# Gathers one expert earlier in the queue, roots by a power on GpSimd, and another order of the last norm, in a hybrid decoder trunk

## The chip, the cores and the metric

The kernel runs on one core of one Trainium2 chip. The metric is the device time of one execution in microseconds (us), lower is better. PE is TensorE, DVE is VectorE, ACT is ScalarE, POOL is GpSimd, and SP is SyncE, which here only starts DMAs.

## The reference

One layer over 1024 tokens of 1024 channels: a token mixer, a cross-attention to 256 memory tokens, and a mixture of 16 experts of which each token uses two; a last RMSNorm stands behind. The change touches the norms, the experts and the last norm:

```
def rmsnorm(x, g):
    xf = x.astype(jnp.float32)
    y = xf * lax.rsqrt(jnp.mean(xf * xf, axis=-1, keepdims=True) + EPS)
    return (y * g.astype(jnp.float32)).astype(x.dtype)
...
    weight = g_val * e_val
    eid = g_idx * EXPERTS_PER_GROUP + e_idx
    gate = jnp.sum(jax.nn.one_hot(eid, N_EXPERTS, dtype=jnp.float32) * weight[..., None], axis=1)
    act = jax.nn.silu(jnp.einsum('nd,edf->nef', t, w_e_gate)) * jnp.einsum('nd,edf->nef', t, w_e_up)
    act = act * gate[:, :, None].astype(act.dtype)
    out = jnp.einsum('nef,efd->nd', act, w_e_down)
...
        x = x + gated_branch_mixer(h, w_in[l], conv_a_w[l], conv_a_b[l], ln_a_g[l], ln_a_b[l],
                                   w_a_out[l], w_pool_grp[l], pool_scale[l], conv_c_w[l],
                                   w_c_out[l], w_o[l])
        x = x + memory_cross_attention(rmsnorm(x, norm_x_g[l]), rmsnorm(mem, norm_mem_g[l]),
                                       w_xq[l], w_xkv[l], w_xo[l])
        x = x + hierarchical_moe(rmsnorm(x, norm_ffn_g[l]), w_rg[l], b_rg[l], w_re[l], b_re[l],
                                 w_e_gate[l], w_e_up[l], w_e_down[l])
    return rmsnorm(x, norm_f_g)
```

## The kernel before

All matrix products take float32 operands apart into a high and a low part (`wh` and `wl`, `xh` and `xl`, `aTh` and `aTl`) and add three products. A weight tile comes by SP's queue as `raw`; ACT casts it to `wh` (L114) and DVE, for a few tiles POOL, subtracts to `wl` (L117). These splits go in the order of one list, and `split_to(n)` in the text says how far at that place; `load_to(n)` does the same for the loads. Instructions run on each engine in the order in which the text issues them; nothing is rescheduled.

**Up to about 1050 us** the mixer and the attention run in tiles of 128 tokens, PE nearly without a gap. The norms' square root (`rstd_of`, L166) is a guess by a shift on integers and three Newton rounds, of small operations on DVE or POOL. The last token tile's norm (`add_half`, L1079, and the lines below it) feeds the router, whose choices give each expert its list of tokens (`toki`) and their number (`cnti`).

**Experts.** They run in a fixed order. Expert e has a first block of up to 128 tokens and, where its count is above 128, a second block in the If branch at L1408. The token rows come by an indirect DMA on POOL (`gather_rows`, L1153) from `t_d` into a slot of `merged`. PE transposes them (`xe`, or `xb` for a second block, L1182), ACT and DVE split the transposed rows (`xh`, `xl`), PE multiplies by the gate and up weights (`gu`, or `gub`, 24 matmuls, L1197), ACT and DVE form silu(gate) times up (`sg`, L1255 and L1256), PE transposes that (`at`, L1291), ACT and DVE split it (`aTh`, `aTl`), PE multiplies by the down weights (`y`, `yb`), ACT and DVE scale the result by the token's weight into one of three y slots of `merged` (L1304, L1306), and an indirect DMA of POOL adds those rows to `x2_d` in memory (`add_rows`, L1157). Each scatter-add waits until the one before it has landed. While expert e runs its gate and up products, DVE does six `wl` of a later expert; `next_in(e)` then transposes the rows of expert e+1. `gather_both(e + 3)` stands behind the branch of expert e, and so behind the scatter-adds of that branch on POOL. Five slots hold gathered rows in turn.

**The last two experts and the last norm.** Experts 14 and 15 don't add to memory. After the last scatter-add of expert 13 the eight 128-token tiles of `x2_d` are loaded by SP (`nat`, L1324), squared and summed on ACT (L1328), scaled on DVE (L1336) and written out; the rows of tokens that experts 14 and 15 use are gathered (`rows_in`), get the experts' result added on DVE (`final_add`, L1351), are squared (L1352), scaled (L1361) and written by an indirect DMA over those of `nat` (`rows_out`, L1345). `HOOKS` is a table of which of these steps runs at which place of expert 14 (key -2) and expert 15 (key -1): "end" is behind the expert, "act" behind the transposes of `sg`, "put" behind the result of the expert before, "gate" behind `sgb`, "act1" behind the transposes of `sgb`.

Of the kernel before, what the change touches and what calls it, by code (L numbers as in the profile page):

```python
# [9 lines left out]
F32 = mybir.dt.float32  # L10
# [9 lines left out]
P = 128  # L20
D = 1024
# [108 lines left out]
def kernel(ctx: ExitStack, tc: tile.TileContext, x, mem, rows, cols, w_in, w_ac,  # L130
# [34 lines left out]

    def rstd_of(ss, name, n=1, unit=None, y=None, base=EPS):  # L166
        unit = unit or dve
        pool = small if y is None else mo
        v = pool.tile([P, NT], F32, tag="v", bufs=2, name=f"v_{name}")[:, :n]
        q = pool.tile([P, NT], F32, tag="q", bufs=2, name=f"q_{name}")[:, :n]  # L170
        if y is None:
            y = pool.tile([P, NT], F32, tag="y", bufs=2, name=f"y_{name}")[:, :n]
        yi = y.bitcast(I32)
        dve.tensor_scalar(v, ss, 1.0 / D, base, op0=OP.mult, op1=OP.add)
        dve.tensor_scalar(yi, v.bitcast(I32), 1, None, op0=OP.logical_shift_right)
        dve.tensor_scalar(yi, yi, -1, 0x5F3759DF, op0=OP.mult, op1=OP.add)
        unit.tensor_scalar(v, v, -0.5, None, op0=OP.mult)
        for _ in range(3):
            if n == 1:
                unit.tensor_scalar(q, y, v, y, op0=OP.mult, op1=OP.mult)  # L180
                unit.tensor_scalar(y, q, 1.5, y, op0=OP.add, op1=OP.mult)
            else:
                unit.tensor_tensor(q, y, v, op=OP.mult)
                unit.tensor_tensor(q, q, y, op=OP.mult)
                unit.tensor_scalar(q, q, 1.5, None, op0=OP.add)
                unit.tensor_tensor(y, q, y, op=OP.mult)
        return y
# [69 lines left out]
    def prep_rstd(b, n):  # L257
        rstds[b] = rstd_of(sums[b], b, n, unit=dve if b == "m" else pool_e)

# [861 lines left out]

    SLOTS = {"x": (3, 4, 5, 6, 7), "y": (0, 1, 2), "f": (0, 1, 2, 5)}
    mslots = {"x": 0, "y": 0, "f": 0}

# [44 lines left out]

    def gather_both(e):  # L1170
        if e:
            gather(e, 0)
# [86 lines left out]
    def gate_up_out(e, ps):  # L1259
        ast.split_to(EW + 6 * e + (8 if e else 10))  # L1260
        ast.load_to(EW + 6 * e + 23)
        if e == 0:
            gather_both(2)
        return act_of(ps, f"{e}")

    def next_in(e, ps):
        xs = xs_tile(f"{e + 1}")
        x_in(xg[e + 1, 0], ps, xs)
        return xs

    sg = gate_up_out(0, gu0)
    xs1 = xs_tile("0b")
# [57 lines left out]
    def norm_rstd(t0, t1):  # L1330
        rstd_of(nsum[:, t0:t1], f"n{t0}", t1 - t0, pool_e, nrstd[:, t0:t1])

# [15 lines left out]
    def final_add(ps, e, b):  # L1348
        for h in range(2):
            f = fin[e, b][:, h * 512:(h + 1) * 512]  # L1350
            dve.scalar_tensor_tensor(f, ps[h], w_of_slot(e, b), f, op0=OP.mult, op1=OP.add)  # L1351
            act.activation(fjunk[:, 0:512], f, AF.Square, accum_out=fsum[:, e - NF, b, h:h + 1])  # L1352

    def final_rstd(e, b, unit):
        ss = fsum[:, e - NF, b]
        dve.tensor_tensor(ss[:, 0:1], ss[:, 0:1], ss[:, 1:2], op=OP.add)
        rstd_of(ss[:, 0:1], f"f{e}_{b}", 1, unit, frstd[:, e - NF, b:b + 1])

# [4 lines left out]
    def put(ps, e, b):  # L1363
        if e < NF:
            y_out(ps, e, b)
        else:
            final_add(ps, e, b)
            if b and e < E2:
                final_rstd(e, b, dve)
                final_scale(e, b)  # L1370
# [7 lines left out]
    def first_rows_out():  # L1378
# [15 lines left out]
    for e in range(NE):  # L1394
# [13 lines left out]
        with tc.If(count_of(e, CALC_P + [ET.SP] if end else CALC_P) > P) as cmp:  # L1408
            x_in(xg[e, 1], bank_pair(f"xb{e}"), xs1)
            if last:  # L1410
                down(yps, *last, 0, (0,))
            if e >= NF:
                rows_in(e, 1)
            act_tr(sg, pa, aT)
            hook(e, "act")
            if last and own:
                down(yps, *last, 0, (1,))
                down(yps, *last, 1)
                put(yps, e - 1, 0)
# [210 lines left out]
```

## Time and profile before

| | |
|---|---|
| median of 3 runs | 1354.13 us (1353.12 to 1354.61) |
| the profiled execution: time, span | 1349.84 us, 1348.2 us |
| busy: PE, DVE, ACT, POOL | 1268.7, 811.1, 447.6, 144.9 us |
| mean granted clock of TensorE | 0.974 |
| 100 to 1057 us: PE busy | 946.01 of 957.00 us |
| 1264.7 to 1282.7 us (expert 13): PE busy | 13.59 of 18.00 us |
| 1282.7 to 1294.3 us (expert 14): PE busy | 7.39 of 11.60 us |
| 1321.1 to 1348.2 us (behind PE's end): DVE busy, POOL busy | 13.79 of 27.10, 7.00 of 27.10 us |

The profiled execution is one other than the three timed ones. Its span is what the traces measure; 1.64 us of its time lie around the span. Share of busy time says little by itself: from 100 to 1057 us PE is full, and behind 1321 us it has nothing left to do.

### The profile page before, as it was taken

The numbers are of one execution on the slowest core, as the hardware profiler recorded it, in microseconds if no ns is written. First come the engines' busy times: TensorE is split into PE (matmuls) and PEld (weight loads), VectorE is DVE, ScalarE is ACT, GpSimd is POOL, SyncE is SP. The second block draws the span as 40 slices with busy tenths as digits, with TensorE's granted clock in tenths as the row PEclk, the third lists the DMA queues.
The fourth block names the chain that finished last, engine by engine and source line by source line (L and its number), as shares of the span: only waits on it lengthen the run. The fifth ranks groups of instructions, "written<-read, shape, count | busy, mean of one in ns | idle before, by whom it ended". The sixth has DMA issues, their size and how long they took to land. (4 is left out here: it accounts for less than half of the span.)

```text
span 1348.2 us, 16066 instructions
## 1 busy us (share of the span) xinstructions
PE 1268.7 (94%) x6150; PEld 1054.2 (78%) x6151; DVE 811.1 (60%) x1210; ACT 447.6 (33%) x611; POOL 144.9 (11%) x157
## 2 busy tenths in 40 slices
PE   7999999999999999999999999999999689998871
PEld 7988888888888888888888898887888477776661
DVE  5836787887874356322344554335777767657665
ACT  6511221221111133212132253435312456555571
POOL 2400000000000000000000020011000423212243
PEclk8999999999999999999999999999999799999986
DMA  7641111121111112111153240113434788979773
GB/s 290 214 145 47 39 63 32 52 78 33 50 58 48 48 34 60 42 52 63 32 199 114 94 158 2 57 43 121 137 113 159 259 285 272 271 216 343 243 240 144
DMA packets 46490, 166.83 MB, mean 124 GB/s; under 512 B 5376, under 2 KB 6144, under 8 KB 46400
## 3 DMA queue, kind: packets, MB, share of 16 engines
q1 hardware_dynamic: 40032, 142.84, 30.8%
q0 software_dynamic: 6224, 22.29, 6.8%
q8 instruction: 54, 0.88, 0.3%
q10 hardware_dynamic: 144, 0.52, 0.1%
q14 instruction: 36, 0.29, 0.1%
HBM read 134.70 MB, written 30.93 MB: 123 GB/s over the span
## 5 line engine op out<-in xcount | busy, mean ns | idle before, releaser
L117 DVE TENSOR_TENSOR wl<-raw,wh 128x1024 fp32r<-128x1024 f32 (+1 forms) x179 | 213.5, 1228 | 145.7 <-ACT wh L114 145.6
L60 PE MATMUL ps<-hTh,wh 128*128 128x512 f32 x768 | 238.1, 390 | 0.0
L64 PE MATMUL ps<-hTh,wl 128*128 128x512 f32 x768 | 237.8, 389 | 0.0
L62 PE MATMUL ps<-hTl,wh 128*128 128x512 f32 x768 | 237.8, 389 | 0.0
L114 ACT CAST wh<-raw 128x1024 fp32r<-128x1024 f32 x197 | 194.8, 1036 | 97.0 <-PE ps L62 42.2
L60 PEld LDWEIGHTS ps<-hTh,wh 128*128 128x128 f32 x768 | 144.1, 188 | 30.4 <-issue 0.5
L64 PEld LDWEIGHTS ps<-hTh,wl 128*128 128x128 f32 x768 | 144.0, 188 | 30.2 <-DVE wl L117 0.2
L62 PEld LDWEIGHTS ps<-hTl,wh 128*128 128x128 f32 x768 | 144.1, 188 | 29.9
L431 DVE SCALAR_TENSOR_TENSOR conv<-glu,colt,conv 128x1024 f32<-128x1024 f32 x120 | 154.1, 1284 | 3.5
L117 POOL TENSOR_TENSOR wl<-raw,wh 128x1024 fp32r<-128x1024 f32 x18 | 44.2, 2461 | 235.3 <-ACT wh L114 235.3
L1157 POOL DMA_INDIRECT x_d<-merged,toki x20 | 37.9, 1897 | 154.2 <-DVE merged L1304 72.2
L60 PE MATMUL v<-Bh,aht 128*128 128x512 f32 x128 | 43.5, 411 | 0.0
L62 PE MATMUL v<-Bl,aht 128*128 128x512 f32 x128 | 41.0, 391 | 0.0
L64 PE MATMUL v<-Bh,alt 128*128 128x512 f32 x128 | 41.0, 391 | 0.0
L60 PE MATMUL s<-Ah,aht 128*128 128x512 f32 x128 | 40.1, 394 | 0.1
L60 PE MATMUL w<-wh,aht 128*128 128x512 f32 x128 | 40.0, 394 | 0.0
L64 PE MATMUL w<-wh,alt 128*128 128x512 f32 x128 | 39.6, 390 | 0.5 <-DVE alt L202 0.5
L64 PE MATMUL s<-Ah,alt 128*128 128x512 f32 x128 | 39.5, 390 | 0.0
L62 PE MATMUL s<-Al,aht 128*128 128x512 f32 x128 | 39.5, 389 | 0.0
L62 PE MATMUL w<-wl,aht 128*128 128x512 f32 x128 | 39.4, 389 | 0.0
L1197 PE MATMUL gu<-wh,xh 128*128 128x512 f32 x120 | 35.1, 415 | 4.0 <-DVE aTl L202 2.1
L1182 PE MATMUL xe<-ident,merged 128*128 128x128 f32 x128 | 18.9, 294 | 18.8 <-DMA merged<-t_d,toki 15.0
(434 smaller groups left out, 2136.0 us busy)
## 6 DMA issues: line engine op xcount, KB each, us to landing
raw<-in_w_e_dram SPq DMA_DIRECT2D x93, 512.0 KB
raw<-in_w_in_dram SPq DMA_DIRECT2D x48, 512.0 KB
raw<-in_w_kv_dram SPq DMA_DIRECT2D x16, 512.0 KB
x_d<-res SPq DMA_DIRECT2D x16, 512.0 KB
xr<-in_x_dram SPq DMA_DIRECT2D x8, 512.0 KB
raw<-in_w_ac_dram SPq DMA_DIRECT2D x8, 512.0 KB
raw<-in_w_o_dram SPq DMA_DIRECT2D x8, 512.0 KB
res<-in_x_dram SPq DMA_DIRECT2D x8, 512.0 KB
```

Of the source, the lines that this page charges most:

```text
L60: nc.tensor.matmul(o, lhsT=lhs.hi, rhs=r.hi, start=first, stop=False)
L62: nc.tensor.matmul(o, lhsT=lhs.hi, rhs=r.lo, start=False, stop=False)
L64: nc.tensor.matmul(o, lhsT=lhs.lo, rhs=r.hi, start=False, stop=last)
L114: e_hi.copy(hi, raw)
L117: e_lo.tensor_tensor(lo, raw, hi.bitcast(F32), op=OP.subtract)
L431: fillers.append(lambda k=k: dve.scalar_tensor_tensor(conv[i], glu[:, k:k + S], col("conv_w", i * TAPS + k), conv[i], op0=OP.mult, op1=OP. ...
L1157: pool_e.indirect_dma_start(out=x2_d[:, :], out_offset=bass.IndirectOffsetOnAxis(ap=idx, axis=0), in_=ys, in_offset=None, compute_op=OP.add)
L1182: pe.transpose(ps[k // 4][:, k % 4 * P:(k % 4 + 1) * P], src[:, k * P:(k + 1) * P], ident)
L1197: pe.matmul(ps, lhsT=getattr(xs[h], x)[:, k, :], rhs=getattr(w[2 * h + k // 2], y)[:, c0:c0 + 512], start=(h, k, x, y) == (0, 0, "hi", "hi ...
```

## The change

It has five parts. The root becomes two operations on POOL, a multiply-add and a power of -0.5. The gather of an expert's first block goes from behind the branch of the expert three before it to ahead of that branch, right behind the transposes that free its slot, with a list of free slots in place of a fixed turn; that of the second block stays behind the branch. The multiply of the last tile's second half goes from POOL to DVE. The splits and loads of the first experts' weights are issued at other places, behind the forming of the token weights. In the last norm, the squares of tiles 0 to 3 go from behind expert 14 to behind the transposes of expert 15's `sg`, the roots are taken in pairs of tiles, and the squares of the added rows stand apart from the adds.

```
-    def rstd_of(ss, name, n=1, unit=None, y=None, base=EPS):
-        unit = unit or dve
+    def rstd_of(ss, name, n=1, y=None, base=EPS):
...
-        dve.tensor_scalar(v, ss, 1.0 / D, base, op0=OP.mult, op1=OP.add)
-        dve.tensor_scalar(yi, v.bitcast(I32), 1, None, op0=OP.logical_shift_right)
-        dve.tensor_scalar(yi, yi, -1, 0x5F3759DF, op0=OP.mult, op1=OP.add)
-        unit.tensor_scalar(v, v, -0.5, None, op0=OP.mult)
-        for _ in range(3):
-            if n == 1:
-                unit.tensor_scalar(q, y, v, y, op0=OP.mult, op1=OP.mult)
-                unit.tensor_scalar(y, q, 1.5, y, op0=OP.add, op1=OP.mult)
...
+        pool_e.tensor_scalar(v, ss, 1.0 / D, base, op0=OP.mult, op1=OP.add)
+        pool_e.tensor_tensor(y, v, minus_half[:, :n], op=OP.pow)
...
-        pool_e.tensor_tensor(xgr[:, cols(h)], x2[:, cols(h)], grow[:, cols(h)], op=OP.mult)
+        (dve if h else pool_e).tensor_tensor(xgr[:, cols(h)], x2[:, cols(h)], grow[:, cols(h)], op=OP.mult)
...
-    dve.tensor_scalar(ss, ss, 1.0 / D, EPS, op0=OP.mult, op1=OP.add)
+    pool_e.tensor_scalar(ss, ss, 1.0 / D, EPS, op0=OP.mult, op1=OP.add)
...
     def gather(e, b):
-        xg[e, b] = mslot("x")
+        x_slot[e, b] = x_free.pop(0)
+        xg[e, b] = merged[:, x_slot[e, b], :]
         gather_rows(xg[e, b], t_d, e, b)
+
+    def gathered_used(e, b):
+        x_free.append(x_slot[e, b])
...
-    gather_both(0)
-    gather_both(1)
-    ast.split_to(EW + 6)
+    gather_second(0)
+    gather(1, 0)
+    gather_second(1)
...
+    ast.split_to(EW + 6)
     xp = act_split("x0")
...
     x_split(pxe, xs0)
-    ast.split_to(EW + 7)
-    w = [ast.get(EW + q) for q in range(6)]
-    gu0 = gate_up(xs0, w, acc_tile("gu0")[:, 0:512])
     pw3 = pw[:, 0:6 * NE].rearrange("p (b c e) -> p b c e", b=2, c=3)
     dve.tensor_copy(wslot, pw3[:, :, 0, :])
     dve.tensor_tensor(wslot, wslot, pw3[:, :, 1, :], op=OP.add)
     dve.tensor_tensor(wslot, wslot, pw3[:, :, 2, :], op=OP.add)
+    ast.split_to(EW + 10)
+    ast.load_to(EW + 18)
+    w = [ast.get(EW + q) for q in range(6)]
+    gu0 = gate_up(xs0, w, acc_tile("gu0")[:, 0:512])
...
     def next_in(e, ps):
         xs = xs_tile(f"{e + 1}")
         x_in(xg[e + 1, 0], ps, xs)
+        gathered_used(e + 1, 0)
+        if e + 3 <= NE - 1:
+            gather(e + 3, 0)
         return xs
...
     HOOKS = {
-        (-2, "end"): [lambda: norm_squares(0, 1, 2, 3), lambda: rows_in(E2, 0), lambda: norm_rstd(0, 4)],
-        (-1, "act"): [lambda: norm_squares(4)],
-        (-1, "put"): [lambda: norm_squares(5, 6, 7), lambda: norm_scale(0, 1, 2), lambda: norm_rstd(4, 8), lambda: norm_scale(3)],
-        (-1, "gate"): [lambda: final_rstd(E1, 0, pool_e)],
-        (-1, "act1"): [lambda: norm_scale(4, 5, 6, 7), lambda: final_scale(E1, 0), first_rows_out],
-        (-1, "put0"): [lambda: final_rstd(E2, 0, dve)],
+        (-2, "end"): [lambda: rows_in(E2, 0)],
+        (-1, "act"): [lambda: norm_squares(0, 1), lambda: norm_rstd(0, 2), lambda: norm_squares(2, 3), lambda: norm_rstd(2, 4)],
+        (-1, "put"): [lambda: norm_scale(0, 1, 2), lambda: norm_squares(4)],
+        (-1, "gate"): [lambda: norm_squares(5), lambda: norm_rstd(4, 6), lambda: norm_scale(3), lambda: norm_squares(6)],
+        (-1, "act1"): [lambda: norm_squares(7), lambda: norm_rstd(6, 8), lambda: final_squares(E1, 0), lambda: final_rstd(E1, 0),
+                       lambda: norm_scale(4, 5, 6, 7), lambda: final_scale(E1, 0), first_rows_out],
+        (-1, "put0"): [lambda: final_squares(E2, 0), lambda: final_rstd(E2, 0)],
...
-        if e + 3 < E2:
-            gather_both(e + 3)
+        gathered_used(e, 1)
+        if e + 3 <= E2:
+            gather_second(e + 3)
```

POOL's program around the branch of one expert, before: first the scatter-adds of the branch (their three forms are for whole blocks, half blocks and the Else side), then the gather.

```order
L1157 DMA x_d<-merged,toki 1152x1024
L1139 TENSOR_LOAD cnti
L1139 ISA x2
L1147 COMPARE_AND_BRANCH
L1157 DMA x_d<-merged,toki 1152x1024
L1147 UNCONDITIONAL_BRANCH
L1157 DMA x_d<-merged,toki 1152x1024
L1147 UNCONDITIONAL_BRANCH
L1157 DMA x_d<-merged,toki 1152x1024
L1408 ISA
L1408 UNCONDITIONAL_BRANCH
L1153 DMA merged<-t_d,toki 128x1024
```

POOL's program at the same place of the changed kernel, where the lines of the gather and of the scatter-adds have the numbers L1143 and L1147:

```order
L1143 DMA merged<-t_d,toki 128x1024
L1129 TENSOR_LOAD cnti
L1415 COMPARE_AND_BRANCH
L1147 DMA x_d<-merged,toki 1152x1024
L1129 TENSOR_LOAD cnti
L1129 ISA x2
L1137 COMPARE_AND_BRANCH
L1147 DMA x_d<-merged,toki 1152x1024
L1137 UNCONDITIONAL_BRANCH
L1147 DMA x_d<-merged,toki 1152x1024
L1137 UNCONDITIONAL_BRANCH
L1147 DMA x_d<-merged,toki 1152x1024
```

The gather of the expert's first block (128x1024 from `t_d`) stood behind the branch and now stands ahead of it, so no scatter-add of that branch is queued ahead of it any more.

ACT's program where expert 15 begins, before (`nat` are the tiles of the last norm, `sg` and `at` belong to expert 15):

```order
L1328 ACTIVATE fjunk,nsum<-nat_11148 128x1024
L1328 ACTIVATE fjunk,nsum<-nat_11150 128x1024
L1328 ACTIVATE fjunk,nsum<-nat_11152 128x1024
L1328 ACTIVATE fjunk,nsum<-nat_11154 128x1024
L1255 ACTIVATE sg_11401<-gu_11376 128x256
L1139 TENSOR_LOAD cnti
L1408 COMPARE_AND_BRANCH
L1147 UNCONDITIONAL_BRANCH
L201 CAST xh_15_11202<-xb_0_11424 128x512
L201 CAST xh_15_11204<-xb_1_11425 128x512
L201 CAST aTh_11407<-at_11406 128x256
L1328 ACTIVATE fjunk,nsum<-nat_11156 128x1024
```

And in the changed kernel, where `sg` is L1250 and the squares are L1329:

```order
L1250 ACTIVATE sg_11158<-gu_11133 128x256
L1129 TENSOR_LOAD cnti
L1415 COMPARE_AND_BRANCH
L1137 UNCONDITIONAL_BRANCH
L189 CAST xh_15_10990<-xb_0_11181 128x512
L189 CAST xh_15_10992<-xb_1_11182 128x512
L189 CAST aTh_11164<-at_11163 128x256
L1329 ACTIVATE fjunk,nsum<-nat_10936 128x1024
L1329 ACTIVATE fjunk,nsum<-nat_10938 128x1024
L1329 ACTIVATE fjunk,nsum<-nat_10940 128x1024
L1329 ACTIVATE fjunk,nsum<-nat_10942 128x1024
L1329 ACTIVATE fjunk,nsum<-nat_10944 128x1024
```

The four squares that stood ahead of `sg` on ACT now stand behind the cast of `aTh`, and the fifth behind them.

DVE's program near the end of expert 15, before, from the last scale of `nat` on (`ya` and `yb` are expert 15's two results, `frstd` the root of added rows):

```order
L1336 SCALAR_TENSOR_TENSOR nat_11162<-nat_11162,nrstd,grow_7834 128x1024
L1361 SCALAR_TENSOR_TENSOR merged<-merged,frstd,grow_7834 128x1024
L1351 SCALAR_TENSOR_TENSOR merged<-ya_0_11545,wslot,merged 128x512
L1351 SCALAR_TENSOR_TENSOR merged<-ya_1_11546,wslot,merged 128x512
L1356 TENSOR_TENSOR fsum<-fsum 128x1
L174 TENSOR_SCALAR v_f_0_11602<-fsum 128x1
L175 TENSOR_SCALAR frstd<-v_f_0_11602 128x1
L176 TENSOR_SCALAR frstd<-frstd 128x1
L177 TENSOR_SCALAR v_f_0_11602<-v_f_0_11602 128x1
L180 TENSOR_SCALAR q_f_0_11603<-frstd,v_f_0_11602 128x1
L181 TENSOR_SCALAR frstd<-q_f_0_11603,frstd 128x1
L1379 UNCONDITIONAL_BRANCH
```

And in the changed kernel, where the adds are L1352 and the scales of added rows L1366:

```order
L1337 SCALAR_TENSOR_TENSOR nat_10950<-nat_10950,nrstd,grow_7648 128x1024
L1366 SCALAR_TENSOR_TENSOR merged<-merged,frstd,grow_7648 128x1024
L1352 SCALAR_TENSOR_TENSOR merged<-ya_0_11281,wslot,merged 128x512
L1352 SCALAR_TENSOR_TENSOR merged<-ya_1_11282,wslot,merged 128x512
L1352 SCALAR_TENSOR_TENSOR merged<-yb_0_11351,wslot,merged 128x512
L1352 SCALAR_TENSOR_TENSOR merged<-yb_1_11352,wslot,merged 128x512
L1385 UNCONDITIONAL_BRANCH
L1366 SCALAR_TENSOR_TENSOR merged<-merged,frstd,grow_7648 128x1024 x2
```

The steps of the root between the adds of `ya` and of `yb` are gone from DVE; POOL has two operations for each root instead.

## Rows read from the trace of the kernel before

**Rows 1.** Page, part 1: busy time of each engine.
```profile
PE 1268.7 (94%) x6150; PEld 1054.2 (78%) x6151; DVE 811.1 (60%) x1210; ACT 447.6 (33%) x611; POOL 144.9 (11%) x157
```

**Rows 2.** PE's waits from 1055 us on: total, times, longest (us).
```profile
PE xe L1182 <- DMA merged<-t_d,toki: 15.0, 6, 4.4
PE at L1291 <- DVE sg L1256: 5.3, 6, 3.4
...
PE xe L1182 <- DVE wslot L1245: 1.6, 1, 1.6
```

**Rows 3.** Timeline of DVE, start of the kernel.
```profile
47.19 3.39 DVE L262 SCALAR_TENSOR_TENSOR xn<-xr,y,g_mix 128x1024 f32<-128x1024 f32 x1 [0.96 <-POOL y L186]
```

**Rows 4.** Timeline of DVE, last token tile's router: the root's first operation and its reader.
```profile
1043.79 0.21 DVE L174 TENSOR_SCALAR v_v<-ss_v7b,ss_v7a 128x1 f32<-128x1 f32 x1 [0.79 <-ACT xnv L1081]
...
1046.23 0.24 DVE L897 SCALAR_TENSOR_TENSOR lg<-rt,y_v,b_rt 128x20 f32<-128x20 f32 x1
```

**Rows 5.** Timeline of PE in experts 3, 7 and 8: end of gate_up, start of gub.
```profile
1106.61 1.07 PE L1197 MATMUL gu<-wh,xl 128*128 128x512 f32 x4
...
1114.78 1.17 PE L1197 MATMUL gub<-wh,xh 128*128 128x512 f32 x4
...
1170.59 1.07 PE L1197 MATMUL gu<-wh,xl 128*128 128x512 f32 x4
...
1177.44 1.66 PE L1197 MATMUL gub<-wh,xh 128*128 128x512 f32 x4
...
1193.17 1.07 PE L1197 MATMUL gu<-wh,xl 128*128 128x512 f32 x4
...
1198.17 1.18 PE L1197 MATMUL gub<-wh,xh 128*128 128x512 f32 x4
```

**Rows 6.** Timeline of DVE in expert 3.
```profile
1102.90 6.89 DVE L117 TENSOR_TENSOR wl<-raw,wh 128x1024 fp32r<-128x1024 f32 x6
1109.71 0.41 DVE L1256 TENSOR_TENSOR sg<-sg,gu 128x256 f32<-128x256 f32 x1
```

**Rows 7.** Timeline of POOL, expert 10: a scatter-add.
```profile
1224.05 1.67 POOL L1157 DMA_INDIRECT x_d<-merged,toki  x1 [4.69 <-POOLq L1408]
```

**Rows 8.** Timeline of ACT, expert 10's end.
```profile
1233.80 0.69 ACT L1306 ACTIVATE merged<-y,wslot 128x512 f32<-128x512 f32 x1 [3.69 <-DMA x_d<-merged,toki]
```

**Rows 9.** Timeline of PE, experts 13 to 15.
```profile
1274.72 1.94 PE L1182 MATMUL xe<-ident,merged 128*128 128x128 f32 x8 [4.41 <-DMA merged<-t_d,toki]
...
1294.30 2.04 PE L1197 MATMUL gu<-wh,xh 128*128 128x512 f32 x4 [2.11 <-DVE aTl L202]
...
1306.71 0.41 PE L1291 MATMUL at<-ident,sg 128*128 128x128 f32 x2 [3.37 <-DVE sg L1256]
```

**Rows 10.** Timeline of SP's queue: the loads for the last norm.
```profile
1295.59 4.03 SPq L1324 DMA_DIRECT2D nat<-x_d  x8
```

**Rows 11.** Timeline of ACT, expert 15.
```profile
1305.54 0.36 ACT L1255 ACTIVATE sg<-gu 128x256 f32<-128x256 f32 x1
...
1309.29 0.63 ACT L1352 ACTIVATE fjunk<-merged 128x512 bf16<-128x512 f32 x1 [0.71 <-ACT fjunk L1328]
```

**Rows 12.** Timeline of DVE, the end.
```profile
1316.07 0.42 DVE L1256 TENSOR_TENSOR sgb<-sgb,gub 128x256 f32<-128x256 f32 x1
...
1319.41 4.89 DVE L1336 SCALAR_TENSOR_TENSOR nat<-nat,nrstd,grow 128x1024 f32<-128x1024 f32 x4 [0.96 <-POOL nrstd L186]
...
1326.92 1.40 DVE L1351 SCALAR_TENSOR_TENSOR merged<-ya,wslot,merged 128x512 f32<-128x512 f32 x2
...
1336.63 1.28 DVE L1361 SCALAR_TENSOR_TENSOR merged<-merged,frstd,grow 128x1024 f32<-128x1024 f32 x1
```

**Rows 13.** Timeline of POOL, the end.
```profile
1309.03 0.20 POOL L184 TENSOR_TENSOR q_n<-q_n,nrstd 128x4 f32<-128x4 f32 x1
...
1319.67 2.27 POOL L180 TENSOR_SCALAR q_f<-frstd,v_f 128x1 f32<-128x1 f32 x1
...
1338.59 0.90 POOL L1345 DMA_INDIRECT out_dram<-merged,toki  x1 [3.13 <-DVEq L1484]
```

More of the change, by code (lines that the diff above doesn't have):

```diff
@@ L148 @@
     small = ctx.enter_context(tc.tile_pool(name="small", bufs=2))
+    minus_half = small.tile([P, 2 * NT], F32, tag="mh", bufs=1, name="minus_half")
     def acc_tile(name):
@@ L164, in col @@
         return colt[:, c:c + 1]
-    def rstd_of(ss, name, n=1, unit=None, y=None, base=EPS):
-        unit = unit or dve
+    def rstd_of(ss, name, n=1, y=None, base=EPS):
         pool = small if y is None else mo
         v = pool.tile([P, NT], F32, tag="v", bufs=2, name=f"v_{name}")[:, :n]
-        q = pool.tile([P, NT], F32, tag="q", bufs=2, name=f"q_{name}")[:, :n]
         if y is None:
             y = pool.tile([P, NT], F32, tag="y", bufs=2, name=f"y_{name}")[:, :n]
-        yi = y.bitcast(I32)
-        dve.tensor_scalar(v, ss, 1.0 / D, base, op0=OP.mult, op1=OP.add)
-        dve.tensor_scalar(yi, v.bitcast(I32), 1, None, op0=OP.logical_shift_right)
-        dve.tensor_scalar(yi, yi, -1, 0x5F3759DF, op0=OP.mult, op1=OP.add)
-        unit.tensor_scalar(v, v, -0.5, None, op0=OP.mult)
-        for _ in range(3):
-            if n == 1:
-                unit.tensor_scalar(q, y, v, y, op0=OP.mult, op1=OP.mult)
-                unit.tensor_scalar(y, q, 1.5, y, op0=OP.add, op1=OP.mult)
[L182 to L186, printed above, removed]
+        pool_e.tensor_scalar(v, ss, 1.0 / D, base, op0=OP.mult, op1=OP.add)
+        pool_e.tensor_tensor(y, v, minus_half[:, :n], op=OP.pow)
         return y
@@ L240 @@
     dve.memset(epst, EPS)
+    pool_e.memset(minus_half, -0.5)
     st.load_to(3)
@@ L257, in prep_rstd @@
     def prep_rstd(b, n):
-        rstds[b] = rstd_of(sums[b], b, n, unit=dve if b == "m" else pool_e)
+        rstds[b] = rstd_of(sums[b], b, n)
     def prep_scale(key, b, i, g):
@@ L1120 @@
     pe.matmul(pc[:, 0:NE], lhsT=ones, rhs=msum, start=True, stop=True)
-    SLOTS = {"x": (3, 4, 5, 6, 7), "y": (0, 1, 2), "f": (0, 1, 2, 5)}
-    mslots = {"x": 0, "y": 0, "f": 0}
+    SLOTS = {"y": (0, 1, 2), "f": (0, 1, 2)}
+    mslots = {"y": 0, "f": 0}
+    x_free, x_slot = [3, 4, 5, 6, 7], {}
     def mslot(kind):
@@ L1168, with gather_second @@
     dve.tensor_copy(cnti, cntf)
-    def gather_both(e):
-        if e:
-            gather(e, 0)
+    def gather_second(e):
         with tc.If(count_of(e, [ET.Pool]) > P):
             gather(e, 1)
-    gather_both(0)
-    gather_both(1)
-    ast.split_to(EW + 6)
+    gather_second(0)
+    gather(1, 0)
+    gather_second(1)
     def x_tr(src, ps):
@@ L1229 @@
     x_tr(xg[0, 0], pxe)
+    gathered_used(0, 0)
     pw = sm.tile([P, 512], F32, tag="sm", name="pw")
@@ L1259, in gate_up_out @@
     def gate_up_out(e, ps):
-        ast.split_to(EW + 6 * e + (8 if e else 10))
+        if e == 0:
+            gather(2, 0)
+            gather_second(2)
+            return act_of(ps, f"{e}")
+        ast.split_to(EW + 6 * e + 8)
         ast.load_to(EW + 6 * e + 23)
-        if e == 0:
-            gather_both(2)
         return act_of(ps, f"{e}")
@@ L1268, in next_in @@
         x_in(xg[e + 1, 0], ps, xs)
+        gathered_used(e + 1, 0)
+        if e + 3 <= NE - 1:
+            gather(e + 3, 0)
         return xs
+    ast.load_to(EW + 23)
     sg = gate_up_out(0, gu0)
@@ L1330, in norm_rstd @@
     def norm_rstd(t0, t1):
-        rstd_of(nsum[:, t0:t1], f"n{t0}", t1 - t0, pool_e, nrstd[:, t0:t1])
+        rstd_of(nsum[:, t0:t1], f"n{t0}", t1 - t0, nrstd[:, t0:t1])
     def norm_scale(*ts):
@@ L1351, in final_add, with final_squares, final_rstd @@
             dve.scalar_tensor_tensor(f, ps[h], w_of_slot(e, b), f, op0=OP.mult, op1=OP.add)
+    def final_squares(e, b):
+        for h in range(2):
+            f = fin[e, b][:, h * 512:(h + 1) * 512]
             act.activation(fjunk[:, 0:512], f, AF.Square, accum_out=fsum[:, e - NF, b, h:h + 1])
-    def final_rstd(e, b, unit):
+    def final_rstd(e, b):
         ss = fsum[:, e - NF, b]
-        dve.tensor_tensor(ss[:, 0:1], ss[:, 0:1], ss[:, 1:2], op=OP.add)
-        rstd_of(ss[:, 0:1], f"f{e}_{b}", 1, unit, frstd[:, e - NF, b:b + 1])
+        pool_e.tensor_scalar(ss[:, 0:1], ss[:, 0:1], 1.0 / D, EPS, op0=OP.mult, op1=OP.add)
+        rstd_of(ss[:, 1:2], f"f{e}_{b}", 1, frstd[:, e - NF, b:b + 1], base=ss[:, 0:1])
     def final_scale(e, b):
@@ L1368, in put @@
             if b and e < E2:
-                final_rstd(e, b, dve)
+                final_squares(e, b)
+                final_rstd(e, b)
                 final_scale(e, b)
@@ L1420 @@
             hook(e, "put")
-            x_slot = mslots["x"]
-            if e == NF - 1:
-                gather_both(e + 2)
             gu1 = gate_up(xs1, w, bank_tile(f"gub{e}"))
@@ L1447 @@
             if end:
+                final_squares(e, 1)
+                final_rstd(e, 1)
                 hook(e, "late")
-                final_rstd(e, 1, dve)
                 final_scale(e, 1)
@@ L1460 @@
             hook(e, "put")
-            if e == NF - 1:
-                mslots["x"] = x_slot
-                gather_both(e + 2)
             hook(e, "gate")
@@ L1472 @@
             hook(e, "late")
-        if e + 3 < E2:
-            gather_both(e + 3)
+        gathered_used(e, 1)
+        if e + 3 <= E2:
+            gather_second(e + 3)
+        if e == NF - 1:
+            SLOTS["f"] += (x_slot[e, 1],)
         ast.split_to(EW + 6 * e + 12)
```

## The prediction

> **What bounds the kernel now.** I read the page first: PE is busy for 94% of the span [rows 1]. From 100 to 1057 us it has 946 of 957 us, so a change can give nothing there, and what it makes slower there costs nothing while it stays beside the products. I then listed PE's waits from 1055 us on, where the experts run [rows 2]. Two groups lead: 15.0 us in six waits of `xe` for gathered rows, the longest 4.4, and 5.3 us of `at` for DVE's `sg`. The third place is behind PE's end: in the last 27 us PE has no work, and DVE and POOL alternate.
>
> Two limits stand close behind the gathers. DVE does six `wl` in 6.89 us while PE does the gate and up products, and `sg` follows only at 1109.71, 2.2 us behind the end of those products [rows 5, 6]. And the scatter-adds go one by one, each behind the landing of the one before: expert 10's stretch shows one issued at 1224.05, and ACT waiting 3.69 us, until 1233.80, for its landing to free a y slot [rows 7, 8]. A gather that comes earlier uncovers these.
>
> **The change part by part.**
>
> *Roots, from DVE or POOL to two operations on POOL.* At the kernel's start the scale of the first `xn` (47.19) waits 0.96 us for the root's last step on POOL [rows 3]. With two operations in place of sixteen the wait goes: **1.0 us**. The last token tile's root takes from 1043.79 to its reader at 1046.23, 2.4 us [rows 4]; two operations might take 0.6, but the router's last products end close behind, so I take **0.7**, between 0 and 1.8. The roots between lie where PE is full, and are hidden by its products. No power is in the trace. From below, a POOL operation on two tensors of 128x4 takes 0.20 us; from above, one beside DVE's scales takes 2.27 [rows 13]. I take 0.6 for a whole root, near the lower row, since operations on a few columns all stand near it when DVE is not at work, and keep 4.5 (twice 2.27) as the other end.
>
> Here a rule speaks against the change. The row shows a single-column operation of 2.27 us on POOL in the very stretch in which DVE scales four tiles for 4.89 us [rows 12, 13]. The Trainium skill ("SBUF — State Buffer", "SBUF: two separate sides") says that a DVE instruction with two inputs in SBUF and a GpSimd instruction that reads SBUF exclude each other for the whole instruction; the trace agrees with it, and by it each POOL root in the last norm could wait for a scale of 1.28 us twice, 2.6 us in place of 0.6, and the sum below would be some 4 us smaller with two of them uncovered.
>
> *First experts' splits.* The wait of `xe` for `wslot` of 1.6 us [rows 2] sits ahead of expert 1, but DVE's `wl` that are moved have to be done by the same expert, so I take **0.5**, between 0 and 1.6.
>
> *Gathers one place earlier.* Every gather of a first block is issued ahead of one expert's scatter-adds in place of behind them. Each costs POOL the same issue as before; what is behind it is those scatter-adds, which get some 1 us later where POOL has the data already (they mostly wait for DVE or for a landing, so this is hidden). What PE gains is not the whole wait. Expert 8 has no wait for a gather, and its second products start at 1198.17, 4.1 us behind the end of its first (1193.17 + about 0.9) [rows 5]: that is the time that `sg` on DVE sets. In expert 3 the same distance is 7.3 us, in expert 7 6.0 us (first products' last four begin at 1106.61 and 1170.59, second products at 1114.78 and 1177.44, the four taking 0.9). So expert 3 gains 3.2 and expert 7 1.9; expert 7's first four second products take 1.66 in place of 1.18 after the gap, which adds 0.4. Together **5.5**. In expert 10 a wait goes too, but ACT stands until the landing at 1233.80 in any case [rows 8], and the next gate and up products need its `wh`: **0**.
>
> Expert 13 is the largest: 4.41 us for `xe` [rows 9]. Its gain meets the y slot and the chain of scatter-adds at once, and in expert 14 DVE's `aTl` is late by 2.11. Between 0 (the chain of scatter-adds lets nothing through) and 4.4 (the whole wait) I take **2.5** for the start of expert 15's products (1294.30 before).
>
> *The last norm.* The loads of `nat` are issued from 1295.59 [rows 10], when the last scatter-add has landed; I count no gain for them, since that scatter-add waits for one landing after the other. But four squares no longer stand ahead of `sg`: ACT's `sg` began at 1305.54 [rows 11], and PE waited 3.37 us for it at `at` [rows 9]. The products end earlier than the tiles land, so the whole wait goes: **3.4**.
>
> Behind DVE's `sgb` (1316.07) the last row DMA is issued at 1338.59, 22.5 us later [rows 12, 13]. In the new order DVE has `sgb` 0.42, one scale 1.28, `aTlb` 0.42, four scales 4.89, the scale of expert 14's rows 1.28, four adds 2.80 and two scales 2.56, 13.65 us in all [rows 12]. To this I add 1.0 for the last squares (0.63 each [rows 11]) and root behind the last add, which the scale of the other block partly covers, 1.0 for the root of tiles 6 and 7, which comes behind ACT's eighth square, and 0.7 to the issue: 16.3. That gives **6.2**. The rest, from the last issue to the span's end, I leave at its 9.6 us (1348.2 less 1338.59). If ACT's squares or the landings of `nat` run late instead, half of this is gone; if no root is uncovered, it is 8.2.
>
> **The sum**: 1.0 + 0.7 + 0.5 + 5.5 + 2.5 + 3.4 + 6.2 = 19.8 us. The profiled execution took 1349.84 and its span 1348.2, with 1.64 around it, so it would take 1330.0. The median of the three runs shown is 1354.13, 4.3 above that execution; taken off it, the forecast is **1334 us**.
>
> **The rivals.**
>
> *All waits for gathers become time.* For it: DVE does the `wl` for later experts, and the order in which it meets them can shift with PE. Against it: expert 8, which has no such wait and still needs 4.1 us where the work between is the eight plus eight transposes and three products. It would add to the 8.0 us from gathers the rest of the 15.0: 27 us, **1327**.
>
> *The last norm gives half.* For it: the loads of `nat` start at the same time, all eight squares are now behind them on ACT, and 4 MB go out while the last rows do; the root in pairs has to pass POOL four times. Then 3.4 + 6.2 shrinks to 4, and the gathers give 5: 1.0 + 0.7 + 0.5 + 5 + 4 = 11, **1343**.
>
> *Nothing to be measured.* The chain of scatter-adds binds from expert 2 to the end, and the loads of `nat` with it: then each gain on PE is lost at the next y slot, and the tail starts when it did. Against it: the waits for y slots are seen at expert 10 alone with any size. **1352 to 1356**.
>
> *Slower, by the power.* Five roots stand uncovered in the new kernel: the first tile's, the last tile's, that of tiles 6 and 7, and expert 15's two. If a root costs x us more than my 0.6, the loss is 5x; it eats the 19.8 us at x = 4.0. Two operations at the slowest row, 2.27 each, make x = 3.9, so nothing is gained. A power that is a routine on POOL of 3 us or more per operation, or that waits for DVE's scales on top, decides for slower: at x = 6 the loss is 30 us and the time 1364. Against it: other operations of few columns on POOL cost 0.2 to 0.3 us when DVE leaves it alone [rows 13]. A rule of the Trainium skill stands on this side too ("GPSIMD Engine Reference", "Engine selection"): two-input elementwise work is about twice as slow on GpSimd as on VectorE. By it a root would be near 1.0, and the time some 2 us later; no row here has both engines at one such operation.
>
> **How the numbers follow.** My forecast has a chance of 0.58, all waits for gathers 0.13, half the last norm 0.16, nothing to be measured 0.06, slower 0.07. A change within 0.2% (2.7 us) is about what a measurement of this kernel can't tell from none. So faster is 0.87, same 0.06, slower 0.07. The likeliest case alone runs from 1328 to 1340: the gathers between 5 and 10 us, the last norm between 6 and 13. The range from 1323 to 1347 takes in the first two rivals with their own spread, and leaves out the last two and the fringes.
>
> **What would show it.** In the new trace: no wait of `xe` for a gather over 1 us in experts 3, 7 and 13, and `at` or `xb` waiting for DVE's `sg` in their place by 1 to 2 us; ACT's wait at expert 10's y slot still there; the `nat` loads issued no more than 1 us earlier against the end of expert 13's last scatter-add; no wait of `at` in expert 15; some 16 us from `sgb` to the last issue; powers on POOL of 0.2 to 0.5 us where DVE is idle. The prediction is wrong if a power takes over 2 us, if the scatter-adds get later by the gathers ahead of them, or if SP's loads of `nat` come later than 1295.6 less the gains before them.

## The result, and the profile after

The changed kernel takes 1338.25 us in the median of four runs (1335.94 to 1339.86), against 1353.62 for the kernel before (1351.45 to 1354.61): a ratio of 0.9888 with a 95% interval from 0.9867 to 0.9909, or 15 us faster. The forecast was 1334, its range 1323 to 1347. The two profiled executions differ by less, 1349.84 to 1339.86, spans 1348.2 to 1338.2. This is the first thing to learn here: the profiled execution of before was 3.8 us quicker than that kernel's median, that of after 1.6 us slower. A second trace of the kernel before, further below, shows a part of why.

PE's waits from 1040 us on, in the changed kernel (total, times, longest in us):

```profile
PE gu L1189 <- ACT wh L114: 7.0, 2, 5.6
PE xb L1174 <- DVE sg L1251: 5.2, 4, 1.3
...
PE gu L1189 <- ACT merged L1307: 3.5, 1, 3.5
PE yb L60 <- ACT aThb L189: 2.9, 1, 2.9
PE xe L1174 <- DMA merged<-t_d,toki: 2.6, 1, 2.6
```

Of the 15.0 us in six waits for gathers [rows 2] one of 2.6 is left, that of the first expert. In their place `xb` waits four times for DVE's `sg`, 1.3 us each, and `gu` waits for `wh` and for a y slot. PE in experts 3 and 7, to be held against [rows 5]:

```profile
1104.62 1.07 PE L1189 MATMUL gu<-wh,xl 128*128 128x512 f32 x4
...
1108.29 0.63 PE L1174 MATMUL xb<-ident,merged 128*128 128x128 f32 x4 [1.28 <-DVE sg L1251]
...
1109.59 1.17 PE L1189 MATMUL gub<-wh,xh 128*128 128x512 f32 x4
...
1164.80 1.07 PE L1189 MATMUL gu<-wh,xl 128*128 128x512 f32 x4
...
1169.79 1.17 PE L1189 MATMUL gub<-wh,xh 128*128 128x512 f32 x4
```

From the last four first products to the second products it is now 4.97 and 4.99 us, where it was 8.17 and 6.85, and expert 8 had 5.00. The products of experts 4, 6 and 8 start 5.2, 5.8 and 8.2 us earlier than in the trace of before.

ACT at the y slots of experts 10 and 13, the counterpart of [rows 8]:

```profile
1227.25 0.69 ACT L1307 ACTIVATE merged<-y,wslot 128x512 f32<-128x512 f32 x1 [7.58 <-DMA x_d<-merged,toki]
...
1273.11 0.69 ACT L1307 ACTIVATE merged<-y,wslot 128x512 f32<-128x512 f32 x1 [5.88 <-DMA x_d<-merged,toki]
```

The first of these waits was 3.69 us and is 7.58 now. The scatter-add that holds its slot, to be held against [rows 7], shows what is lost:

```profile
1215.97 2.70 POOL L1147 DMA_INDIRECT x_d<-merged,toki  x1 [4.80 <-POOLq L1415]
```

It is issued 8.1 us earlier than in the trace of before, but ACT goes on only 6.6 us earlier (1227.25, was 1233.80): the slot comes free 11.3 us behind the issue, where it was 9.8. What the gathers give in expert 10 and 1.6 us more is spent here, and the products of expert 12 start 6.6 us earlier, not 8.2.

The loads of the last norm on SP's queue, the counterpart of [rows 10], and ACT in expert 15:

```profile
1288.63 4.03 SPq L1325 DMA_DIRECT2D nat<-x_d  x8
```

```profile
1292.06 0.39 ACT L1250 ACTIVATE sg<-gu 128x256 f32<-128x256 f32 x1 [4.57 <-issue]
...
1298.96 1.06 ACT L1329 ACTIVATE fjunk<-nat 128x1024 bf16<-128x1024 f32 x1 [1.33 <-DMA nat<-x_d]
...
1302.12 1.06 ACT L1329 ACTIVATE fjunk<-nat 128x1024 bf16<-128x1024 f32 x1 [2.00 <-DMA nat<-x_d]
...
1303.18 0.37 ACT L1250 ACTIVATE sgb<-gub 128x256 f32<-128x256 f32 x1
1303.99 1.06 ACT L1329 ACTIVATE fjunk<-nat 128x1024 bf16<-128x1024 f32 x1 [0.44 <-DMA nat<-x_d]
...
1306.05 1.06 ACT L1329 ACTIVATE fjunk<-nat 128x1024 bf16<-128x1024 f32 x1 [0.91 <-DMA nat<-x_d]
...
1307.10 0.35 ACT L189 CAST aThb<-atb 128x256 fp32r<-128x256 f32 x1
```

`sg` is no longer behind the squares, and PE has no wait at `at`. But the squares of tiles 3, 4, 5 and 6 wait for their tiles (4.7 us in all), and `aThb` stands behind tile 6's square: PE's `yb` waits 2.9 us for it. The DMA engines show what the tiles wait for (windows of 5 us: PE, PEld, DVE, ACT and POOL busy, granted clock, DMA share, GB/s):

```profile
1290.00:1295.00 5.00, 5.00 (x28) 4.19 (x27) 2.04 (x4) 2.62 (x5) 2.06 (x3) 1.00 1.00 369
1295.00:1300.00 5.00, 5.00 (x23) 4.12 (x22) 1.91 (x3) 3.60 (x8) 0.92 (x2) 1.00 1.04 383
...
1305.00:1310.00 5.00, 2.49 (x11) 2.01 (x12) 2.81 (x4) 4.03 (x11) 2.21 (x4) 1.00 1.01 411
1310.00:1315.00 5.00, 0.52 (x3) 0.09 (x1) 3.61 (x4) 0.02 (x1) 3.87 (x4) 0.80 0.94 377
1315.00:1320.00 5.00, 0.00 (x0) 0.00 (x0) 3.10 (x5) 2.89 (x8) 1.67 (x4) 0.50 0.21 82
```

From 1290 to 1315 us all sixteen DMA engines are full (share 0.94 to 1.04). POOL has the roots and the row DMAs:

```profile
1296.82 0.73 POOL L174 TENSOR_TENSOR nrstd<-v_n,minus_half 128x2 f32<-128x2 f32 x1
...
1309.24 1.61 POOL L174 TENSOR_TENSOR nrstd<-v_n,minus_half 128x2 f32<-128x2 f32 x1
1310.93 1.29 POOL L1361 TENSOR_SCALAR fsum<-fsum 128x1 f32<-128x1 f32 x1
1312.33 1.17 POOL L173 TENSOR_SCALAR v_f<-fsum 128x1 f32<-128x1 f32 x1
1313.58 0.56 POOL L174 TENSOR_TENSOR frstd<-v_f,minus_half 128x1 f32<-128x1 f32 x1
...
1322.98 2.08 POOL L1346 DMA_INDIRECT out_dram<-merged,toki  x1 [0.18 <-issue]
1328.60 0.90 POOL L1346 DMA_INDIRECT out_dram<-merged,toki  x1 [3.54 <-DMA out_dram<-merged,toki]
```

A power on two columns takes 0.73 us where DVE is idle (0.55 to 0.57 on one column), and 1.61 beside DVE's scales; a plain multiply-add of one column beside them 1.17 to 1.29. The last row DMA waits 3.54 us for the landing of the one before. From `sgb` (1303.69) to the last issue it is 24.9 us; before, it was 22.5, and the forecast had 16.3.

### The profile page after: what moved, and what is told of

It is laid out like the page before. It is cut to its first block, busy times and chain, and to the rows that moved or that the text cites. A ratio compares the mean times of both kernels' runs of the same rounds, so it can differ in the third digit from the quotient of the medians.

```text
span 1338.2 us, 15877 instructions
## 1 busy us (share of the span) xinstructions
PE 1265.0 (95%) x6150; PEld 1051.8 (79%) x6151; DVE 769.6 (58%) x996; ACT 447.3 (33%) x611; POOL 148.2 (11%) x154
## 5 line engine op out<-in xcount | busy, mean ns | idle before, releaser
L1147 POOL DMA_INDIRECT x_d<-merged,toki x20 | 38.1, 1907 | 138.7 <-DVE merged L1305 52.2
L190 DVE TENSOR_TENSOR alt<-merged,aht 128x1024 fp32r<-128x1024 f32 (+1 forms) x25 | 30.4, 1220 | 13.1 <-ACT aht L189 13.1
```

Of the source, the lines that this page charges most:

```text
L190: dve.tensor_tensor(dst.lo, src, dst.hi.bitcast(F32), op=OP.subtract)
L1147: pool_e.indirect_dma_start(out=x2_d[:, :], out_offset=bass.IndirectOffsetOnAxis(ap=idx, axis=0), in_=ys, in_offset=None, compute_op=OP.add)
```

## The experiments

All but one are timed in five rounds, and ratios are to the kernel before on the same chip, with 95% intervals.

**Each part alone.** The diff falls into four parts that can be put into the kernel before one by one; together they are the whole change. *The gathers*: the free list and

```
     def next_in(e, ps):
         xs = xs_tile(f"{e + 1}")
         x_in(xg[e + 1, 0], ps, xs)
+        gathered_used(e + 1, 0)
+        if e + 3 <= NE - 1:
+            gather(e + 3, 0)
```

> The kernel before with the earlier gathers alone. Theory A (the gathers give most of the gain, and the new order of the last norm gives back what it takes): expert 15's products start some 7 to 9 us earlier and the loads of the last norm some 6 us earlier, the tail keeps its length, so 7 us faster, ratio 0.995. Theory B (the last norm's order gives most): 3 us or less, ratio 0.998.

Measured: 1349.34 us, 0.9965 (0.9951 to 0.9979), midway between A and B. The trace shows where the rest went. The loads of the last norm start at 1291.51, 4.1 us earlier than before, and expert 15's products at 1287.91, 6.4 us earlier. Then PE waits at `at`:

```profile
1304.64 0.66 PE L1300 MATMUL at<-ident,sg 128*128 128x128 f32 x2 [9.45 <-DVE sg L1261]
...
1305.53 0.63 PE L62 MATMUL y<-wl,aTh 128*128 128x512 f32 x1
...
1308.94 1.09 PE L1201 MATMUL gub<-wh,xh 128*128 128x512 f32 x4
```

The four squares ahead of `sg` wait for their tiles, so the wait of 3.37 us [rows 9] becomes 9.45, and `at` comes only 2.1 us earlier than before. These 2.1 us go right behind it, where the trace of before has

```profile
1307.19 0.40 PE L62 MATMUL y<-wl,aTh 128*128 128x512 f32 x1
```

From `at` to expert 15's second products it was 2.33 us and is 4.30: behind the long wait TensorE's granted clock is 0.50 (1304.9 to 1308.9 us), its level of 1.2 GHz, where before it was 1.00 at the same place (1306.9 to 1309.0 us), its level of 2.4 GHz. So a wait of PE here costs more than its own length.

*The new order of the last norm*: `HOOKS` as in the diff, `final_squares` on its own, with the Newton roots.

> The kernel before with the new order of the last norm alone, the roots still by Newton rounds (pairs of tiles and expert 14's first block on POOL, the other added rows on DVE). Theory A: the wait of 3.4 us for sg goes, and is lost again behind sgb, where ACT's squares wait for the tiles that land late: 0 to 2 us faster, ratio 0.9985 to 1. Theory B: 6 us or more, ratio 0.9955 or lower.

Measured: 1362.36 us, 1.0062 (1.0040 to 1.0084): slower, which neither theory had. Four pairs of tiles mean four Newton roots of sixteen operations each, three on DVE and thirteen on POOL, and DVE's scales wait for them:

```profile
DVE nat L1336 <- POOL nrstd L186: 6.2, 3, 2.9
...
DVE v_n L174 <- ACT fjunk L1328: 3.7, 3, 1.8
DVE fsum L1360 <- ACT fjunk L1356: 2.8, 3, 0.9
DVE merged L1365 <- POOL frstd L181: 2.1, 1, 2.1
```

*The roots by a power*, with the multiply of the last tile's second half on DVE:

```
-        dve.tensor_scalar(v, ss, 1.0 / D, base, op0=OP.mult, op1=OP.add)
...
+        pool_e.tensor_scalar(v, ss, 1.0 / D, base, op0=OP.mult, op1=OP.add)
+        pool_e.tensor_tensor(y, v, minus_half[:, :n], op=OP.pow)
```

> The kernel before with the roots by a power on GpSimd alone, all other order as before. Theory A: 0.4 us at the start, 1 us at the last token tile, and behind expert 15 two roots of 2.4 us on DVE become about 1.3 us on POOL: 3 to 4 us faster, ratio 0.9975. Theory B: as A at the start, and little behind expert 15, since POOL's operations beside DVE's scales take over 1 us each: 1 us, ratio 0.999.

Measured: 1345.03 us, 0.9932 (0.9918 to 0.9946): more than twice what A had, and the largest part. Where it all comes from is shown only in part, as told below.

*The first experts' splits* as in the diff:

> The kernel before with the other places of the first experts' splits and loads alone. Both theories: within 1 us, ratio 0.9993 to 1.0007; expert 0's products start later and expert 1's at the same time or up to 1 us earlier.

Measured: 1352.33 us, 0.9998 (0.9985 to 1.0012). The time is as expected.

**Each part taken out of the changed kernel**, since the four ratios together make only 0.4% of the 1.1% that the change gives.

> The changed kernel with the gathers put back behind the branches. Theory A (the parts need each other: an earlier gather is worth time only where the squares don't stand ahead of sg, and the new order of the last norm only with the short roots): the gathers are worth 6 to 7 us here, so ratio 0.9935 to 0.994. Theory B (the parts add up as they came out alone: roots -9, gathers -5, new order of the last norm +8, splits 0): 1348 to 1353, minus 1, ratio 0.999.

> The changed kernel with the order of the last norm put back. Theory A: the wait of at for sg grows to 9 us, as in the run of the gathers alone, so that the gathers give almost nothing, and the roots alone are left: 1343 to 1345, ratio 0.993. Theory B: without the new order's 8 us it is faster than the changed kernel: 1339 or less, ratio 0.9895 or less.

> The changed kernel with the Newton roots put back (on POOL for the pairs of tiles and expert 14's first block, on DVE for the other added rows). Theory A: slower than before or equal, 1353 to 1358, ratio 1.000 to 1.003, with DVE's sgb and scales behind roots on both engines. Theory B: 1353.3 - 5 + 8 = 1357, ratio 1.003; A and B agree here, and the run gives the price of the roots in the new order: 15 us or more.

Measured: without the gathers 1342.5 us, 0.9919 (0.9897 to 0.9942); without the new order 1342.18, 0.9913 (0.9892 to 0.9935); without the short roots 1356.1, 1.0013 (0.9998 to 1.0029). Against the whole change (0.9888) the roots are worth 1.25%, 17 us, the gathers and the new order 0.3% each, 3 to 4 us, which is hardly more than the uncertainty of such a difference (about 0.3%). The parts don't add up: the new order costs 8 us with Newton roots and gives 3 to 4, at the edge of what is measured, with powers. So B falls, and A is right that the new order needs the short roots. But A is wrong on the gathers: they give about as much in the old order (0.35% alone) as in the new one, and not the 6 to 7 us that A had.

**The kernel before once more**, for a second trace:

> The kernel before once more, for a second trace. The profiled execution of before took 1349.84 us and its runs 1353.3 in the median. If the difference lies in the queues of the expert stretch, this trace shows the start of the last norm's loads at another time than 1295.59, by about as much as its time differs, and the start of the kernel and the tail behind expert 15 alike.

It took 1351.99 us, its span 1350.3. The loads of the last norm start at 1293.85, earlier and not later, and the end comes 3.9 us later behind them, so that expectation was wrong. Half of the 3.9 us is the clock again:

```profile
1306.89 0.66 PE L1291 MATMUL at<-ident,sg 128*128 128x128 f32 x2 [7.14 <-DVE sg L1256]
...
1311.19 1.10 PE L1197 MATMUL gub<-wh,xh 128*128 128x512 f32 x4
```

From `at` to the second products it takes 4.30 us, at a granted clock of 0.50, in place of 2.33. Among the 54 timed runs of the kernel before, the 19 with a mean granted clock of 0.977 or more took 1352.1 us in the mean and the 11 with 0.974 or less 1355.5, so the time of one kernel's executions goes with the clock, too. The start of the kernel isn't alike either, and shows what the first trace had missed. PE's waits of the first 75 us there, and in the changed kernel:

```profile
PE tr_m L276 <- DMA xr_m<-in_mem_dram: 4.9, 2, 4.7
PE tr L197 <- DVE xn L262: 3.2, 2, 1.8
```

```profile
PE tr_m L265 <- DMA xr_m<-in_mem_dram: 6.3, 2, 4.8
...
PE kv L64 <- DVE wl L117: 1.3, 1, 1.3
```

In five of the six traces with Newton roots PE waits twice for `xn` here, 2.7 to 3.2 us in all; the profiled execution of before is the sixth, with one wait of 1.3. In none of the eight with powers does it wait. The mixer's first large products start at 68.9 to 71.1 us in the six, 70.3 in the mean, and at 67.3 to 69.3 in the eight, 68.4 in the mean.

**What holds the rest**, on top of the changed kernel. First the y slots: the kernel deals them in the order of the text, in which the two branches of the If have three calls, so that every Else branch gets the same slot.

```
     def y_out(ps, e, b):
-        ys = mslot("y")
+        ys = merged[:, 2 if b else e % 2, :]
```

> The changed kernel with the y slots dealt otherwise: results of first blocks go to slots 0 and 1 in turn, those of second blocks to slot 2, so that a result no longer waits for the landing of the scatter-add just issued from the same slot. Theory A (the y slot is what holds experts 10 and 13, and what is gained there comes out at the end): ACT's waits of 7.6 and 5.9 us go, PE's waits of 5.6 and 3.5 us go, the loads of the last norm are issued 5 to 9 us earlier: 1330 to 1333. Theory B (the scatter-adds' landings one after the other set the start of those loads whatever the slots do): the waits go, the loads start within 2 us of before: 1336 to 1338.

Measured: 1329.32 us, 0.9816 (0.9793 to 0.9838): A, and faster than both kernels. PE's wait of 5.6 us and ACT's of 7.6 are gone, the other two stay (3.6 and 6.0, at expert 13), and the loads start 12.2 us earlier in the trace, where the runs gain 9. Of the 12.2 us 3.4 are there at expert 1's second products already (1076.14 in place of 1079.50), ahead of the first wait for a slot; some 9 are left for the slots:

```profile
1276.38 3.92 SPq L1325 DMA_DIRECT2D nat<-x_d  x8
```

Then expert 13's own result too, whose slot still waited:

```
-        ys = merged[:, 2 if b else e % 2, :]
+        ys = merged[:, 2 if b or e == NF - 1 else e % 2, :]
```

> The kernel with the y slots dealt otherwise, and expert 13's own result in slot 2 as well, whose last scatter-add landed long before. Theory A (the loads of the last norm start when the last scatter-add has landed, and the end follows that start by 49 to 50 us in every kernel with the new order and the short roots): PE's wait of 3.6 us ahead of expert 14 goes, but the scatter-adds of experts 12 and 13 still go one behind the other's landing, so the loads start within 1 us of the same time against expert 12's scatter-add: 1328 to 1330, no gain. Theory B (the end follows PE): 3 us faster, 1326.

Measured: 1329.97 us, 0.9816 (0.9791 to 0.9841): A. Expert 15's products start at 1270.98 in place of 1274.79, but the loads no earlier (3.3 us later in this trace; against expert 12's scatter-add 1.6 us later, where A had 1), and the time is the same:

```profile
1279.69 3.71 SPq L1325 DMA_DIRECT2D nat<-x_d  x8
```

*ACT's squares in another order*:

```
-        (-1, "put"): [lambda: norm_scale(0, 1, 2), lambda: norm_squares(4)],
-        (-1, "gate"): [lambda: norm_squares(5), lambda: norm_rstd(4, 6), lambda: norm_scale(3), lambda: norm_squares(6)],
-        (-1, "act1"): [lambda: norm_squares(7), lambda: norm_rstd(6, 8), lambda: final_squares(E1, 0), lambda: final_rstd(E1, 0),
+        (-1, "put"): [lambda: norm_scale(0, 1, 2)],
+        (-1, "gate"): [lambda: norm_squares(4), lambda: norm_scale(3)],
+        (-1, "act1"): [lambda: norm_squares(5), lambda: norm_rstd(4, 6), lambda: norm_squares(6, 7), lambda: norm_rstd(6, 8),
+                       lambda: final_squares(E1, 0), lambda: final_rstd(E1, 0),
```

> The changed kernel with ACT's squares in expert 15 moved back: tile 4 behind sgb, tiles 5 and 6 behind aThb. Theory A (in the last norm the eight tiles' way through the DMA engines sets the end, PE's late yb costs nothing): PE's wait of 2.9 us for aThb goes, the last issue comes within 1 us of the same time: 1337 to 1339. Theory B (squares that wait for a tile hold aThb, and with it DVE's queue, which sets the end): 2 to 3 us faster, 1335.5.

Measured: 1338.37 us, 0.9884 (0.9863 to 0.9905): A. `yb` waits 0.46 us for `aThb` in place of 2.9, and the time is that of the changed kernel.

*One row DMA less*:

```
-        (-1, "late"): [lambda: final_scale(E2, 0), lambda: rows_out(out, E2, 0)],
+        (-1, "late"): [lambda: final_scale(E2, 0)],
```

> The changed kernel without the row DMA of expert 15's first block (its 128 rows are left as the last norm wrote them, so this part of the output is left out). Theory A (behind the last scale the two row DMAs go one after the other, each behind the landing of the one before, and that is the end now): the last row DMA follows the last scale at once, 4 us earlier: ratio to the changed kernel 0.997. Theory B (the last scale sets the end, as before the change): within 1 us.

Measured: 1335.76 us, 0.9853 (0.9831 to 0.9876), which is 2.5 us by the medians and 4.7 by the ratios, in line with A. The last row DMA now follows the last scale:

```profile
1323.31 1.28 DVE L1366 SCALAR_TENSOR_TENSOR merged<-merged,frstd,grow 128x1024 f32<-128x1024 f32 x1 [1.08 <-POOL frstd L174]
```

```profile
1324.88 0.99 POOL L1346 DMA_INDIRECT out_dram<-merged,toki  x1 [1.61 <-DVE merged L1366]
```

**One number puts the tails in order**: the time from the first load of the last norm to the end of the span, in each trace.

| kernel | first load | span | between |
|---|---|---|---|
| before, both traces | 1295.59, 1293.85 | 1348.2, 1350.3 | 52.6, 56.5 |
| gathers alone | 1291.51 | 1348.1 | 56.6 |
| splits alone | 1295.47 | 1349.5 | 54.0 |
| roots alone; changed, old order | 1292.91; 1287.69 | 1346.7; 1341.4 | 53.8; 53.7 |
| new order alone; changed, Newton roots | 1299.03; 1292.64 | 1364.3; 1357.6 | 65.3; 65.0 |
| changed | 1288.63 | 1338.2 | 49.6 |
| changed, old gathers | 1290.66 | 1340.3 | 49.6 |
| changed, ACT's squares later | 1285.68 | 1335.0 | 49.3 |
| y slots; with expert 13's | 1276.38; 1279.69 | 1325.6; 1328.3 | 49.2; 48.6 |
| one row DMA less | 1289.07 | 1334.6 | 45.5 |

With the new order and the powers, and all three row DMAs, the end follows those loads by 48.6 to 49.6 us, whatever PE does: the last four of expert 15's second gate and up products start between 8.1 and 14.1 us behind the loads. In the old order PE's `sg` stood between, so an earlier load was not all gain. There the end follows `sgb`: from it to the last issue it is 22.5 us in each of the four traces with Newton roots, and 20.5 and 20.8 in the two with powers.

## Why the prediction was right, and where not

The time lies in the range, on the side that was forecast, 4 us from the forecast; the likeliest case (1328 to 1340) holds it. Its terms did not all hold, and that the sum came out near is in part luck: in the two first traces the terms make 10 us in place of 19.8, and the 15 us of the runs lie nearer only since these two executions were a quick one of the kernel before and a slow one of the changed kernel.

- **The root at the start, 1.0.** The mechanism is right, the size was off: 1.9 us in the means above. The profiled execution had one of the two waits that the five other traces with Newton roots have; one trace was taken for the kernel.
- **The last token tile's root, 0.7.** From `rt` to the last `rk` it is 5.83 us in both traces of before and 5.11 in that of the changed kernel: 0.72. The first expert's rows come no earlier for it (1057.24 before, 1057.52 after), since POOL issues their gather 1.5 to 1.8 us behind the start of `toki` in the eight traces with powers and 0.5 to 0.8 us in the six with Newton roots; why is open.
- **The price of a power.** 0.55 to 0.73 us and a multiply-add of 0.19 to 0.27 where DVE is idle: 0.9 for a root, in place of 0.6; beside DVE's scales up to 2.2. The rival "slower, by the power" would have needed x = 4.0. This is what the Trainium skill's rule ("SBUF — State Buffer", "SBUF: two separate sides") gives, and the rows agree: the slow ones stand beside two-input work of DVE.
- **The splits, 0.5.** Nothing, within the interval.
- **The gathers, 5.5.** 6.2 us from expert 3 to expert 8 in the two traces, and DVE's `sg` is next, as said; 0.6 of it comes from expert 5, whose wait of 1.87 us I had left out. Expert 10 gave nothing, as said, and took back 1.6 us of what had been gained.
- **Experts 13 and 14, 2.5.** The lead of expert 15's products grows by 3.0 us from expert 13 on, with the y slot's wait of 3.5 in it.
- **The wait of `at` for `sg`, 3.4.** Gone; the lead at the second products of expert 15 is 3.7 us larger than at its first.
- **Behind `sgb`, 6.2. This step failed.** I added up DVE's work there, 13.65 us with 2.7 for what no work covers, and left the loads of `nat` out as gaining nothing. But the stretch follows those loads: `sgb` came 12.4 us earlier and the loads 5 to 7, so 24.9 us passed in place of 16.3. Of the 8.6 us that I missed, 3.8 lie between the end of the last scale (1324.1) and the last issue, where I had 0.7 and the last row DMA waits for a landing; the rest lies ahead of that scale, where squares wait for tiles and POOL's roots take up to 1.6 us an operation beside DVE's scales. How it divides between these two is not shown. The rival "the last norm gives half" named this place. On the other side the loads were not fixed: they come 5 to 7 us earlier, since the scatter-adds of experts 12 and 13 do. From the loads to the end the change takes 3.0 us off the one trace of before and 6.9 off the other.
- **The rest behind the last issue, 9.6**: 9.6 again. But the last issue itself now waits for a landing, which was hidden behind DVE before; without it the tail of the trace is 4 us shorter.

The terms as measured in the two first traces (2.0 at expert 2, 6.2 by expert 8, less 1.6 by expert 12, then 3.0, 3.7, less 0.9 at `sgb` behind a square, less 2.4 behind it) make 10, the difference of the spans. The runs say 15. The 5 between are the 3.8 us by which that execution of before was quick and the 1.6 by which that of the changed kernel was slow. Two things that this trace of before lacks are in the second one: the longer wait for `xn` (1.9 us more) and the lower clock behind `at` (2.0 us). That the roots alone give 8 us is shown only in part: the traces have 1.9 at the start and 1.7 to 2.0 between `sgb` and the last issue, and the rest is open. The six runs of that kernel had a mean granted clock of 0.980 in the median, those of before 0.976, so a part may be the clock; no run tells how much. The pair that differs in the roots and the splits alone (the gathers alone against the changed kernel with the old order, spans 1348.1 and 1341.4) puts 3.8 us of its 6.7 ahead of the loads and 2.9 behind.

## What to carry to other kernels

When the last stage begins with a reload that waits for the last write, time that stage from its first load, not from the engine that looks busy; work moved ahead of it on other engines is worth what it takes off that start. Cut a root or any small serial chain short before splitting the work that needs it into pieces: the same order cost 8 us with the long chain and gave 3 to 4, hardly clear of the noise, with the short one. And slots dealt by a count in the text aren't dealt in the order of the run where branches share the text: one line that dealt three slots by hand gave 9 us more than the change.

## What the chip showed that I had not expected

A power on GpSimd over one or two columns costs 0.55 to 0.73 us, some three times a multiply-add there; beside DVE's scales the one takes up to 1.6 and the other up to 1.3. Two row DMAs into the same tensor go one behind the other's landing, 5.6 us from issue to issue. And one execution can miss what another of the same kernel has: 1.3 us of waits for `xn` against 3.2 (2.7 to 3.2 in the five other traces with Newton roots), and a granted clock of 1.00 against 0.50 for the products behind `at`, where PE had waited 3.37 us in the one and 7.14 in the other.
